# Two adaLN blocks of a trunk's down projection moved to general slots, and two low parts moved behind a mixing stage

## The chip, the cores and the metric

The kernel runs on one core of a Trainium2 chip. Its engines work side by side, each on its own list of instructions, in an order that is fixed when the program is built: PE multiplies matrices, DVE (vector) and ACT (scalar) do the work element by element, POOL does a few memsets and DMA issues, SP issues nearly all DMAs. They wait for each other through semaphores. The metric is the device time of one execution in microseconds; lower is better. All times below are in us unless they say ns.

## What is computed

A trunk of two layers over 512 tokens of width 1024. Layer 0 mixes tokens by a stick-breaking attention, layer 1 by a gated MLP that mixes positions inside chunks. Each mixer is followed by a SwiGLU FFN (width 2816), and each of the four sub-layers is wrapped in norms that a conditioning vector `c` shifts, scales and gates (adaLN):

```python
def ada_modulation(c, w, b):
    m = jax.nn.silu(c) @ w + b
    shift, scale, gate = jnp.split(m, 3, axis=-1)
    return shift[:, None, :], scale[:, None, :], gate[:, None, :]
...
def token_mixing_mixer(h, w_in, ln_g, w_s, b_s, w_out):
    uv = jax.nn.gelu(h @ w_in)
    u, v = jnp.split(uv, 2, axis=-1)
    v = layer_norm(v, ln_g)
    ...
    sv = jnp.einsum('gts,bnsgc->bntgc', ws, v) + b_s.T[None, None, :, :, None]
    y = u * sv.reshape(B, S, D)
    return y @ w_out

def swiglu(h, w_gate, w_up, w_down):
    return (jax.nn.silu(h @ w_gate) * (h @ w_up)) @ w_down
...
    for i in range(DEPTH):
        shift, scale, gate = ada_modulation(c, mix_ada_w[i], mix_ada_b[i])
        h = rms_norm(x, mix_pre_g[i]) * (1.0 + scale) + shift
        ...
        x = x + gate * rms_norm(y, mix_post_g[i])
        shift, scale, gate = ada_modulation(c, ffn_ada_w[i], ffn_ada_b[i])
        h = rms_norm(x, ffn_pre_g[i]) * (1.0 + scale) + shift
        y = swiglu(h, ffn_w_gate[i], ffn_w_up[i], ffn_w_down[i])
        x = x + gate * rms_norm(y, ffn_post_g[i])
```

## The kernel before

**Numbers in two parts.** Every fp32 operand is split into a high part that PE takes as it is (`wh`, `hTh`, `as`'s first half) and a low part, the rest (`wl`, `hTl`). A product is three matmuls: high by high, high by low, low by high (`mm3`). ACT makes the high part by a copy, DVE the low part by a subtraction, so each weight block costs one operation on either engine.

**Stages.** Attention; its output projection; gate and up of FFN0; the down projection of FFN0 (22 blocks `f` of 128 rows, each for 4 token tiles and 2 halves of the width); the mixing layer (`gmlp`); gate, up and down of FFN1. Each projection back to the width is `out_proj`: it loops over the blocks, the last four of them (the tail) per token tile, and after each tile `boundary` does the residual, the norms and the transposes (`tp`) for the next stage. In the first down projection, the sums of token tile 0 are set aside after block `mid - 1` (`yp`, `mid` = 13), because PSUM banks are needed.

**Weights.** `stream` lists all weight blocks in the order of use. `wload` issues the DMA of one into `raw` (2 buffers), `wemit` splits it into `wh`, `wl` (6 buffers), `wget` takes it. Gate and up columns of most FFN blocks, and two pairs of columns of the mixing layer's `u`, are computed with seven products in place of eight; their weights come as two loads, `rawx` (in `raw`) and `rawy` (in `raw2`, another pool of 2 buffers), and `blocks` (L255 on) builds sums of them, among others `b21`, a high and a low part of half of `rawy`.

**adaLN.** A `Bg` object spreads the matrix-vector products of adaLN over other work. Its name A, B or G stands for scale, shift and gate, the figure for the sub-layer. Each step issues one 512 KB load of ada weights (`rawada`) and, `lag` steps later, one multiply-add on DVE that uses it. After eight such products per part, the sum is split, PE adds over the partitions by a matmul with ones (`adaps`) and the row of norm gains `g` is put on. With `slots` of 0 the loads go to `raw2`; otherwise they go to the general slots, a pool of 28 tiles of 4 KB per partition (`slot`) that nearly everything else lives in as well. With `flat`, the parts follow each other without a pause to drain the lag.

In the first down projection two of them run: `bg` (A1, B1 and G2, in general slots, two steps per block, done by block 12) and `bg2` (A2 and B2, in `raw2`, lag 1). A2 and B2 are needed only at the boundary after the mixing layer; their last part (`adaps`) is done inside that layer.

**The mixing layer.** It computes `v` and `u`, normalises `v` (the statistics end in `r`, the variable `normed`), and for each of eight groups m: `sv` matmuls on PE, four `svt` operations on DVE, one product with `u`, and a split into `as`, on which the first output products (`part`) run. While it does so, weights of what follows are prepared.

**Order.** Inside the gate and up stages the order on PE, DVE and ACT is written out (`chain`). Elsewhere, a scheduler at build time sets the order on each engine from the program's order as priority, readiness and free buffers; an operation far back in the program may go early when its inputs and a buffer are there. `order(b, before)` keeps `b` behind another operation of the same engine without a semaphore. The low part of `b21` has such an order: for the `u` pairs behind the last sum of `v`'s weights (`summed`), for the first blocks of FFN1 behind `normed`.

The lines that the change and the prediction's steps touch: the low part of `b21` (L297 to L299), the steps of `bg2` in `out_proj` (L653, L654), `yp` (L656), `normed` (L1615), the end of the mixes (L1678 to L1681), and the making of `bg2` (L1694).

Of the kernel before, what the change touches and what calls it, by code (L numbers as in the profile page):

```python
# [15 lines left out]
NT = T // P  # L16
# [19 lines left out]
def trunk(ctx: ExitStack, tc: tile.TileContext, A: dict, out: bass.AP):  # L36
# [17 lines left out]
    def nm(s):  # L54
        uid[0] += 1
        return f"{s}_{uid[0]}"

    def slot(dt, name, a=2, b=512):
        return s4.tile([P, a, b], dt, tag="s4", name=nm(name))
# [21 lines left out]
    dve = Vector()  # L81
# [21 lines left out]
    def order(b, before):  # L103
        tc.add_manual_dep(
            b.ins, before.ins.name,
            mybir.DependencyInfo(mybir.DependencyClass.NoSync, mybir.DependencyReason.DATA),
            reason="order",
        )
# [28 lines left out]
    stream = []  # L137
    got = []
# [1 line left out]
    wpools = [(wpool, 5)]  # L140
    fwork = {}
    last_low = [None]
    last_block, summed, normed = [None], [None], [None]

    raws = []

# [43 lines left out]
    def wtile(a, b, at=0):  # L190
        turn[0] = (turn[0] + 1) % sum(c for _, c in wpools)
        pool = wpools[0][0] if turn[0] < wpools[0][1] else wpools[1][0]
        if at is SHORT:
            at = SHORT[turn[0] % 2]
        return [
            pool.tile([P, 1088], F32R, tag=n, name=nm(n))[:, at : at + a * b].rearrange(
                "p (a b) -> p a b", a=a
            )
            for n in ("wh", "wl")
        ]  # L200
# [57 lines left out]
    def blocks(xr, yr):  # L258

        fp = fwork["pool"]  # L260

        def high(t, src):
            act.activation(t[0][:], src, AF.Copy)

        def low(t, src):
            return dve.tensor_tensor(t[1][:], src, t[0][:].bitcast(F32), ALU.subtract)

        def half(t, i):
            return lambda k: (t[0][:, 4 * i + k, :], t[1][:, 4 * i + k, :])

        x = wtile(KD, P, SHORT)
        high(x, xr[:])
        f13 = fp.tile([P, KD, P], F32, tag="f13", name=nm("f13"))
        sum13 = dve.tensor_tensor(
            f13[:].rearrange("p (a k) f -> p a (k f)", a=2),
            xr[:].rearrange("p (a k) f -> p a (k f)", a=2),
            yr[:, 4:8, :].rearrange("p (a k) f -> p a (k f)", a=1).to_broadcast([P, 2, 512]),
            ALU.add,
        )
        if len(got) == first_blocks[-1]:  # L280
            order(sum13, feature[0])
        yield
        b21 = [
            fp.tile([P, 544], F32R, tag=f"b21{i}", name=nm("b21"))[
                :, SHORT[0] : SHORT[0] + 512
            ].rearrange("p (a b) -> p a b", a=4)
            for i in range(2)
        ]
        high(b21, yr[:, 0:4, :])
        t13 = wtile(KD, P, SHORT)  # L290
        high(t13, f13[:])
        f24 = fp.tile([P, KD, P], F32, tag="f24", bufs=1, name=nm("f24"))
        dve.tensor_tensor(f24[:, 0:4, :], f13[:, 0:4, :], xr[:, 4:8, :], ALU.add)
        dve.tensor_tensor(f24[:, 4:8, :], f24[:, 0:4, :], yr[:, 0:4, :], ALU.add)
        yield
        low(x, xr[:])
        b = low(b21, yr[:, 0:4, :])  # L297
        if normed[0] is not None:
            order(b, (summed if stream[len(got)][3][1][0] == "u" else normed)[0])  # L299
        yield  # L300
        t24 = wtile(KD, P, SHORT)
        high(t24, f24[:])
        low(t13, f13[:])
        yield
        low(t24, f24[:])
        got.append({
            "B11": half(x, 0), "B22": half(x, 1), "B21": half(b21, 0),
            "T1": half(t13, 0), "T3": half(t13, 1), "T2": half(t24, 0), "T4": half(t24, 1),
        })
# [308 lines left out]
    def out_proj(s, nk, get_act, wkey, J, bg, hT, nxt=(), pre=None, S=None, steps=0, bg2=None):  # L618

        last = 0 if steps else 3
        mid = min(nk - J, -(-8 * len(bg.parts) // steps) + 1) if steps else None
        yp = None
        y = [[None, None] for _ in range(NT)]

        def step(k, tt, a, w, halves=(0, 1)):
            for hf in halves:  # L630
                if k == 0 or k == mid and tt == last:
                    y[tt][hf] = bank("y", "p" if tt == last else "b")
                mm3(
                    y[tt][hf][:],
                    a[0][:, tt * P : (tt + 1) * P], a[1][:, tt * P : (tt + 1) * P],
                    w[0][:, 0, hf * 512 : (hf + 1) * 512],
                    w[1][:, 0, hf * 512 : (hf + 1) * 512],
                    k == 0 or k == mid and tt == last, k == nk - 1 or k + 1 == mid and tt == last,
                )

        npre = 0
        if pre is not None:
            npre = len(pre["w"])
            for tt in pre["y"]:
                y[tt] = pre["y"][tt]
        for k in range(nk - J):
            a = get_act(k)
            w = pre["w"][k] if k < npre else wget(wkey(k))
            for tt in range(NT):
                if k >= npre or tt not in pre["y"]:  # L650
                    step(k, tt, a, w)
            bg.step(steps)
            if bg2 is not None and k >= mid - 3 and k != mid - 1:  # L653
                bg2.step(4 if k < mid else 2)  # L654
            if k + 1 == mid:
                yp = slot(F32, "yp")  # L656
                for hf in range(2):
                    act.activation(yp[:, hf, :], y[last][hf][:], AF.Copy)
                bg.step(99)
        bg.step(99)  # L660
        tail = [
            (k, get_act(k), wget(wkey(k), J + 1 if k == nk - J else 0))
            for k in range(nk - J, nk)
        ]
        sqrt_table()
        xs = {tt: x_load(tt) for tt in range(2)}
        xin = xs.get
        for tt in range(NT):
            for hf in range(2):
                for k, a, w in tail:  # L670
                    step(k, tt, a, w, (hf,))
            if tt == last and yp is not None:
                for hf in range(2):
                    dve.tensor_tensor(yp[:, hf, :], y[tt][hf][:], yp[:, hf, :], ALU.add)
                y[tt] = [yp[:, hf, :] for hf in range(2)]
            if tt < 2:
                boundary(s, tt, y[tt], xin, hT, S, "p" if last == 0 else "b")
                xs[tt + 2] = x_load(tt + 2)
        evacs, late = [], []
        for n, tt in enumerate((2, 3)):  # L680
            def mid():
                edge[0] = True
                evacs.append(nxt[1]())
                edge[0] = False

            if nxt and tt == 2:
                evacs.append(nxt[0]())
            late.append(
                boundary(
                    s, tt, y[tt], xin, hT, S, "p" if tt == 3 else "b",  # L690
                    mid if nxt and tt == 3 else None,
                )
            )
        if nxt:
            evacs.append(nxt[2]())
            with tc.issue_after(last_sqrt[0].ins):
                for f in evacs:
                    f()
        if hT is not None:
            for f in late:  # L700
                f()
# [201 lines left out]
    with tc.tile_pool(name="att", bufs=1) as att, tc.tile_pool(name="att2", bufs=2) as att2:  # L903
# [58 lines left out]
        B31, B2, B0 = (3, 1), (2,), (0,)  # L962
# [582 lines left out]
    def gmlp(bg, hT, nhT, nS, nxt):  # L1545
# [66 lines left out]
        sd = small.tile([P, 52], F32, tag="sd4", bufs=1, name=nm("sd4"))[:, :NT]  # L1612
        act.activation(sd, mv[:, :, 1], AF.Sqrt, bias=epsb[:])
        r = small2.tile([P, 48], F32, tag="r4", bufs=1, name=nm("r4"))
        normed[0] = dve.reciprocal(r[:, :NT], sd)  # L1615
        vn = []
        for tt in range(NT):
            dve.tensor_scalar(
# [31 lines left out]
        def part(k):  # L1650

            w = wget(("wout", k), 2)
            pre["w"].append(w)
            for tt, y in pre["y"].items():
                for hf in range(2):
                    if k == 0:
                        y[hf] = bank("y", "p" if tt == 3 else "b")
                    c = slice(hf * 512, (hf + 1) * 512)
                    tok = slice(tt * P, (tt + 1) * P)
                    mm3(  # L1660
                        y[hf][:], sp[k][0][:, tok], sp[k][1][:, tok],
                        w[0][:, 0, c], w[1][:, 0, c], k == 0, False,
                    )
# [14 lines left out]
        for m in range(3, KD):  # L1678
            mixed(m)
            if m > 3:  # L1680
                part(m - 4)  # L1681
        out_proj(
            2, KD, lambda k: sp[k], lambda k: ("wout", k), 4, bg, nhT, nxt, pre, nS,
        )
# [6 lines left out]
        0, KD, lambda k: (o8[k][:, 0, :], o8[k][:, 1, :]), lambda k: ("wo", k),  # L1691
        4, bg, hT1, f0.first(), early, S1,
    )
    bg2 = Bg("A2", "B2", lag=1, gap=3)  # L1694
    f0.run(
        Bg("G1", slots=1), Bg("A1", "B1", "G2", slots=3, lag=2, flat=True), bg2, 2, hT2,
        [lambda: v_first(hT2, (0, 1)), lambda: v_first(hT2, (2, 3)), lambda: u_first(hT2)], S2,
# [107 lines left out]
```

## Time and profile before

| | us |
|---|---|
| median of 3 runs | 1103.92 |
| lowest and highest run | 1100.98, 1109.13 |
| the profiled execution | 1103.49 |
| its span, first to last instruction | 1101.7 |

The mean granted clock of PE in the profiled execution is 0.998 of full speed. Its stages, read from the profile's table of windows:

| stage | from, to | PE busy | DVE busy | DMA share |
|---|---|---|---|---|
| start and attention | 0 to 245 | 234.0 | 203.5 | 0.82, then 0.36 |
| output projection | 245 to 278 | 32.9 | 24.1 | 0.36 |
| FFN0 gate and up | 278 to 497 | 218.4 | 200.2 | 0.43 |
| FFN0 down projection | 497 to 621 | 123.7 | 109.7 | 0.78 |
| mixing layer | 621 to 764 | 142.6 | 126.5 | 0.38 |
| FFN1 gate and up | 764 to 980 | 215.8 | 198.2 | 0.37 |
| FFN1 down projection | 980 to 1101.7 | 114.6 | 110.5 | 0.32 |

How to read the lines below. In the table of windows: from and to, length, then for PE, PEld (weight loads of PE), DVE, ACT and POOL the busy time and in brackets the number of instructions, then the granted clock, the busy share of the DMA engines and GB/s. In a timeline: start, length, engine, line, operation, the tile it writes and those it reads, shape, number of merged instructions, and in square brackets how long the engine had been idle before and what ended that. In the chain that ended last: start, length, engine and tile; it is followed back from the last instruction, at each step to what released it. Matmuls are pipelined, so that PE's pace is read from the distance of their starts, or from their number in a window, rather than from the length of one. A name like `as<-act` is the tile written and the tile read.

### The profile page before, as it was taken

Reading aid. Unit: us, or ns where it says so; the run is one execution under the profiler, and the core shown is the slowest. Engines: PE = TensorE matmul, PEld = TensorE weight load, DVE = VectorE, ACT = ScalarE, POOL = GpSimd, SP = SyncE. Lnnn points to the kernel's source line nnn. Section 1 sums busy time; section 2 is a strip of 40 time slices with the busy share of each in tenths; the row PEclk is TensorE's granted clock in tenths of the full one; section 3 lists DMA queues with packets and bytes.
Section 4 is the critical chain, followed back from the end, with each engine's and each line's share of the span. In section 5 each row is a group of like instructions: output and inputs, shape, how many; then the busy total and the mean of one; then the engine's idle time right before and its main releaser. Section 6 shows DMA issues by size and latency. Waiting matters only on the chain.

```text
span 1101.7 us, 18701 instructions
## 1 busy us (share of the span) xinstructions
PE 1082.1 (98%) x7452; PEld 978.7 (89%) x7452; DVE 972.8 (88%) x1293; ACT 610.1 (55%) x1016; POOL 29.5 (3%) x53
## 2 busy tenths in 40 slices
PE   7999999999999999999999999999999999999997
PEld 4787788788999999998888899988999999999996
DVE  4988999866989999989978999868979999899996
ACT  6554665665655555554252767526545555565662
POOL 0020100000000000001000000001000000000000
PEclk9999999999999999999999999999999999999999
DMA  8976434304433434359878324524334342332252
GB/s 317 357 226 218 138 121 131 122 17 153 153 111 124 163 124 153 134 187 347 294 246 322 143 87 137 177 95 163 122 113 153 136 159 100 107 113 96 77 190 78
DMA packets 51355, 176.38 MB, mean 160 GB/s; under 512 B 6074, under 2 KB 9146, under 8 KB 51268
## 3 DMA queue, kind: packets, MB, share of 16 engines
q1 hardware_dynamic: 48708, 166.81, 43.8%
q0 software_dynamic: 2560, 8.39, 2.1%
q8 instruction: 58, 0.95, 0.3%
q14 instruction: 29, 0.24, 0.1%
HBM read 164.69 MB, written 8.39 MB: 157 GB/s over the span
## 4 chain that ended last, share of the span: by engine, by line
PE 85%; DVE 7%; DMA 4%; issue 2%; ACT 2%; SPq 0%; DVEq 0%; ACTq 0%
PE r L111 35%; PE y L111 16%; PE pqk L111 7%; PE X L111 4%; PE gu L111 4%; PE Y L111 3%; PE v L111 3%; PE u L111 2%; PE av L111 2%; PE z L111 2%; PE tw L119 1%; PE Z L111 1%; PE W L111 1%; PE tp L119 1%; DVE wl L184 1%
## 5 line engine op out<-in xcount | busy, mean ns | idle before, releaser
L111 PE MATMUL r<-Sh,wh 128*128 128x256 f32 x640 | 177.3, 277 | 0.6 <-ACT e L89 0.6
L111 PE MATMUL r<-Sl,wh 128*128 128x256 f32 x640 | 177.0, 277 | 0.0
L111 PE MATMUL r<-Sh,wl 128*128 128x256 f32 x640 | 176.9, 277 | 0.0
L89 ACT ACTIVATE wh<-raw 128x1024 fp32r<-128x1024 f32 (+1 forms) x105 | 108.3, 1036 | 101.7 <-DMA raw<-in_wdown 36.1
L111 PE MATMUL y<-wh,as 128*128 128x512 f32 x480 | 150.5, 391 | 0.3 <-DVE svt L73 0.3
L111 PEld LDWEIGHTS r<-Sh,wh 128*128 128x128 f32 x640 | 120.2, 188 | 1.2 <-ACT e L89 1.0
L111 PEld LDWEIGHTS r<-Sl,wh 128*128 128x128 f32 x640 | 120.2, 188 | 0.1
L111 PEld LDWEIGHTS r<-Sh,wl 128*128 128x128 f32 x640 | 120.1, 188 | 0.0
L184 DVE TENSOR_TENSOR wl<-raw,wh 128x1024 fp32r<-128x1024 f32 x79 | 95.9, 1220 | 25.9 <-ACT wh L89 25.7
L73 DVE TENSOR_TENSOR wl<-f,wh 128x1024 fp32r<-128x1024 f32 x95 | 112.9, 1219 | 1.1 <-ACT wh L89 1.1
L89 ACT ACTIVATE wh<-f 128x1024 fp32r<-128x1024 f32 x95 | 100.2, 1055 | 17.3 <-DVE f L73 12.5
L111 PEld LDWEIGHTS y<-wh,as 128*128 128x128 f32 x480 | 90.0, 188 | 19.3 <-issue 0.6
L89 ACT ACTIVATE e<-r 128x256 f32<-128x256 f32 x120 | 45.9, 384 | 102.3 <-PE r L111 100.2
L111 PE MATMUL y<-wl,as 128*128 128x512 f32 x240 | 93.7, 391 | 0.0
L111 PE MATMUL r<-hTh,wh 128*128 128x256 f32 x320 | 88.8, 278 | 0.2 <-DVE gu L73 0.2
L111 PE MATMUL r<-hTh,wl 128*128 128x256 f32 x320 | 88.5, 277 | 0.0
L111 PE MATMUL r<-hTl,wh 128*128 128x256 f32 x320 | 88.5, 277 | 0.0
L111 PEld LDWEIGHTS r<-hTh,wh 128*128 128x128 f32 x320 | 60.1, 188 | 1.1 <-DVE gu L73 0.9
L111 PE MATMUL r<-hTh,b 128*128 128x256 f32 x320 | 60.9, 277 | 0.0
L111 PEld LDWEIGHTS r<-hTl,wh 128*128 128x128 f32 x320 | 60.1, 188 | 0.0
L111 PEld LDWEIGHTS r<-hTh,wl 128*128 128x128 f32 x320 | 60.1, 188 | 0.0
L89 ACT ACTIVATE wh<-rawx 128x1024 fp32r<-128x1024 f32 x40 | 42.5, 1062 | 29.7 <-PE r L111 28.9
(288 smaller groups left out, 2924.3 us busy)
## 6 DMA issues: line engine op xcount, KB each, us to landing
rawada<-in_ada SPq DMA_DIRECT2D x80, 512.0 KB, 6.3
rawy<-in_wy SPq DMA_DIRECT2D x38, 512.0 KB, 4.2
rawx<-in_wx SPq DMA_DIRECT2D x38, 512.0 KB, 3.4
raw<-in_wdown SPq DMA_DIRECT2D x22, 512.0 KB, 5.3
raw<-in_wdn SPq DMA_DIRECT2D x22, 512.0 KB, 3.4
raw<-in_wqk SPq DMA_DIRECT2D x16, 512.0 KB, 4.0
ada<-in_ada0p SPq DMA_DIRECT2D x12, 512.0 KB, 7.6
raw<-in_wgu SPq DMA_DIRECT2D x12, 512.0 KB, 3.5
```

Of the source, the lines that this page charges most:

```text
L73: b = getattr(nc.vector, op)(*args, **kw)
L89: b = nc.scalar.activation(*args, **kw)
L111: b = nc.tensor.matmul(o, l, r, start=start, stop=stop, skip_group_check=True)
L119: last_tp[0] = nc.tensor.transpose(o, i, ident)
L184: last_low[0] = nc.vector.tensor_tensor(l[:], raw[:], h[:].bitcast(F32), ALU.subtract)
```

## The change

Two things are changed.

1. `bg2` (A2, B2) gets `slots=2, lag=2, flat=True`: its loads go to general slots, each product comes two steps after its load, and B2 follows A2 without a pause. Its 18 steps run at blocks 9 to 15 (1, 3, 3, 2, 3, 3, 3) and no longer at blocks 10, 11 (4 each) and 13 to 17 (2 each).
2. The low parts of `b21` of FFN1's blocks are ordered behind the last DVE operation of the mixes (`mixes`), and no longer behind the statistics of `v` (`normed`). The `u` pairs keep their order.

```diff
-    last_block, summed, normed = [None], [None], [None]
+    last_block, summed, mixes = [None], [None], [None]
...
         b = low(b21, yr[:, 0:4, :])
-        if normed[0] is not None:
-            order(b, (summed if stream[len(got)][3][1][0] == "u" else normed)[0])
+        after = summed if stream[len(got)][3][1][0] == "u" else mixes
+        if after[0] is not None:
+            order(b, after[0])
...
             bg.step(steps)
-            if bg2 is not None and k >= mid - 3 and k != mid - 1:
-                bg2.step(4 if k < mid else 2)
+            if bg2 is not None and mid - 4 <= k < mid + 3:
+                bg2.step((1, 3, 3, 2, 3, 3, 3)[k - mid + 4])
...
-        normed[0] = dve.reciprocal(r[:, :NT], sd)
+        dve.reciprocal(r[:, :NT], sd)
...
             if m > 3:
                 part(m - 4)
+        mixes[0] = dve.prev
         out_proj(
...
-    bg2 = Bg("A2", "B2", lag=1, gap=3)
+    bg2 = Bg("A2", "B2", slots=2, lag=2, gap=3, flat=True)
```

## The prediction

> **What bounds the kernel now.** I read the page first, then the table of windows, then the chain that ended last, then the timelines around its stops.
>
> ```profile
> span 1101.7 us, 18701 instructions
> ...
> PE 1082.1 (98%) x7452; PEld 978.7 (89%) x7452; DVE 972.8 (88%) x1293; ACT 610.1 (55%) x1016; POOL 29.5 (3%) x53
> ```
>
> PE is busy for 98% of the span, so only its few gaps, and any stretch where its matmuls come slower than they could, can be won. The change works in the first down projection (about 496 to 621 us) and in the mixing of the next layer (about 697 to 730 us). The 20 us windows of the down projection, where x is the number of matmuls on PE:
>
> ```profile
> 500.00:520.00 20.00, 20.00 (x90) 16.58 (x89) 19.77 (x19) 7.91 (x11) 0.95 (x1) 1.00 0.92 334
> 520.00:540.00 20.00, 20.00 (x90) 16.58 (x89) 18.89 (x19) 6.39 (x9) 1.79 (x2) 1.00 0.94 348
> 540.00:560.00 20.00, 20.00 (x90) 16.57 (x89) 17.47 (x15) 3.95 (x5) 0.12 (x1) 1.00 0.76 263
> 560.00:580.00 20.00, 20.00 (x88) 16.18 (x87) 15.78 (x22) 12.60 (x21) 0.00 (x0) 1.00 0.65 221
> 580.00:600.00 20.00, 20.00 (x90) 16.57 (x89) 16.13 (x16) 5.32 (x5) 0.00 (x0) 1.00 0.89 315
> 600.00:620.00 20.00, 19.74 (x96) 16.09 (x95) 18.28 (x29) 13.16 (x33) 1.61 (x3) 1.00 0.47 181
> ```
>
> PE starts 90 matmuls per 20 us, 0.222 us each, whether DVE is busy 19.77 or 16.13 us of a window and whether DMA is at 0.94 or 0.76: here it waits for nobody. One block f of the projection is 4 token tiles x 2 halves x 3 products = 24 matmuls, 24 x 0.222 = 5.33 us. The chain leaves PE in this stage all the same, because it ends in a late transpose:
>
> ```profile
> 598.11 0.06 DVE B L73
> 598.17 1.14 issue
> 599.31 1.23 DVE wl L184
> 600.55 0.33 SPq L128
> 600.88 0.05 issue
> 600.93 4.36 DMA rawy<-in_wuy
> 605.32 0.64 ACT b L89
> 605.95 1.05 ACT junk L89 x2
> ...
> 608.89 1.09 PE tp L119 x8
> ```
>
> Read upwards: the first token tile's transposes (tp) wait for its norm, the norm for the sum of squares on ACT (junk), that stands behind the rounding of b21 (b), which waits for rawy; on SP rawy stood behind a load that waited for a weight's low part (wl), and that ran on DVE after the last B2 product, which held the raw2 buffer that rawy takes. How much of that PE feels:
>
> ```profile
> 607.79 0.62 PE L111 MATMUL y<-wh,as 128*128 128x512 f32 x2
> 608.24 0.39 PE L111 MATMUL y<-wl,as 128*128 128x512 f32 x1
> 608.89 1.09 PE L119 MATMUL tp<-identt,t 128*128 128x128 f32 x8 [0.26 <-DVE t L73]
> ```
>
> Two matmuls start from 607.79 to 608.24, 0.225 us each; the one at 608.24 takes 0.65 us to the next start, so PE lost 0.65 - 0.225 = 0.42 us.
>
> **The change, part by part.**
>
> *A2/B2 (L654, L1694).* The 18 steps (16 loads and 16 multiply-adds, with the lag) stay 18; they go from f = 10, 11, 13 to 17 to f = 9 to 15. So 16 loads on SP, 16 DVE operations, two POOL memsets and two bias loads are neither added nor removed. The last product moves two blocks forward, 2 x 5.33 = 10.7 us, from 598.11 to about 587. DVE has room for that: it idles 20 - 17.47, 20 - 15.78 and 20 - 16.13, together 10.6 us, between 540 and 600. PE doesn't follow (its rate above), so this shift in itself is worth nothing; its cover is that weights and operands are ready ahead, and if the cover goes the price is that of the rivals.
>
> *raw2 freed.* A2/B2 no longer use the two raw2 buffers, so the two rawy loads of the u pairs can go any time after the first gate/up stage, and their two b21 roundings on ACT leave the boundary. What that is worth comes from these rows of DVE and ACT:
>
> ```profile
> 604.10 1.28 DVE L73 SCALAR_TENSOR_TENSOR x<-t,r,x 128x1024 f32<-128x1024 f32 x1
> ```
> ```profile
> 605.32 0.64 ACT L89 ACTIVATE b<-rawy 128x512 fp32r<-128x512 f32 x1 [1.45 <-DMA rawy<-in_wuy]
> 605.85 1.04 ACT L89 ACTIVATE junk<-x 128x1024 bf16<-128x1024 f32 x1
> ```
>
> x was there at 604.10 + 1.28 = 605.38; junk began at 605.85, 0.47 us late, for b alone. Without b the transposes could start at 608.89 - 0.47 = 608.42, before the matmul of 608.24 has given way (608.47): the whole 0.42 us goes. More can't be won here, for PE comes to the transposes only then; late next is PE's own order. The two rawy loads land earlier among the down weights: 2 x 0.524 MB at the 348 GB/s of the full window is 3.0 us, covered by the weights' lead (11.8 us for f = 17, rival C). In general slots the 16 ada loads are bounded by slots, not by raw2, and no row shows how SP would use that; bounds: -0.42 us (wait gone) to rival C's +3.3.
>
> *b21 lows behind the last mix (L298, L1682).* Two DVE operations of 0.68 us move, nothing is added but the order.
>
> ```profile
> 691.62 0.68 DVE L73 TENSOR_TENSOR b<-rawy,b 128x512 fp32r<-128x512 f32 x1
> ...
> 696.29 0.68 DVE L73 TENSOR_TENSOR b<-rawy,b 128x512 fp32r<-128x512 f32 x1
> 697.36 0.48 DVE L73 SCALAR_TENSOR_TENSOR svt<-sv,cols,bsb 128x256 f32<-128x256 f32 x1 [0.38 <-PE sv L111]
> ...
> 731.92 1.23 DVE L184 TENSOR_TENSOR wl<-raw,wh 128x1024 fp32r<-128x1024 f32 x1 [1.79 <-ACT wh L89]
> ```
>
> These are FFN1's two. After the second DVE still waited 0.38 us for PE before the first mix, so the lows stood in nobody's way: I take 0. At their new place DVE idles 1.79 us before one operation; two lows, 1.36 us, fit in it. Queued behind them there are the low parts of the wout weights; the waiting costs them nothing while that idle time lasts. Best case, from PE's rows in the mixing:
>
> ```profile
> 713.85 0.39 PE L111 MATMUL y<-wh,as 128*128 128x512 f32 x1
> 714.49 0.47 PE L111 MATMUL y<-wh,as 128*128 128x512 f32 x1 [0.26 <-DVE svt L73]
> ```
>
> 0.64 - 0.225 = 0.42 us lost to DVE; at best it goes. Worst case the two lows land in front of the next boundary: +1.36 us. The range keeps both; 0 is nearer to the row of 697.36.
>
> **Sum.** -0.42 + 0 + 0 = -0.4 us. The profiled execution took 1103.49 us for its span of 1101.7; it becomes 1103.1. The median shown, 1103.92, is 0.43 above it, so the median becomes 1103.5.
>
> **A rule against the row.** The Trainium skill's "Perfetto Trace Analysis", section "Identifying the Most-Contended Engine", holds matmul busy time for a poor measure and points to the share of LDWEIGHTS: here 16.58 of 20 us, 83%, which read as headroom leaves 17% in this stage. The trace does not agree: three windows in a row have exactly 90 matmuls, with different loads on DVE and DMA. That reading is rival D below.
>
> **Rivals.**
>
> *A. Nothing to measure.* The wait for b21 goes, but the scheduler, with other loads in front, puts another small ACT or DVE operation there; 0.4 us returns: 1103.9.
>
> *B. A late operand.* The operand of block 13 is the tightest of the stage.
>
> ```profile
> 557.75 2.60 DVE L73 SCALAR_TENSOR_TENSOR A<-rawada,sc,A 128x1024 f32<-128x1024 f32 x2
> 563.41 2.50 DVE L73 TENSOR_TENSOR as<-act,as 128x512 fp32r<-128x512 f32 x4 [3.07 <-ACT as L89]
> ...
> 576.60 1.22 DVE L184 TENSOR_TENSOR wl<-raw,wh 128x1024 fp32r<-128x1024 f32 x1
> ```
> ```profile
> 561.58 1.28 ACT L89 ACTIVATE yp<-y 128x512 f32<-128x512 f32 x2 [5.01 <-PE y L111]
> ```
>
> yp starts when PE has finished tile 0 of block 12; three tiles, 18 x 0.222 = 4.0 us, remain, so block 13 starts about 565.6. The first of the four lows is done at 563.41 + 0.68 = 564.1: a lead of 1.5 us. A product of A2 in front of it, as step f = 12 has two where it had none, costs 2.60 / 2 = 1.30 us; DVE's idle 3.07 us and the lead cover 4.6 us. Six of them in front, 7.8 us, delay PE by 3.2 us: 1107.1. For it: 1.5 us is little. Against: six more at one place is much.
>
> *C. Slower: a burst of ada loads.* With general slots nothing but free slots holds SP back. At 348 GB/s a 512 KB load takes 0.524 / 0.348 = 1.51 us. Block 17's weights are ready at 576.60 + 1.22 = 577.8; PE needs them four blocks after block 13 began, with the 12 broadcast matmuls of A1, B1 and G2 between: 565.6 + 4 x 5.33 + 12 x 0.222 = 589.6, a lead of 11.8 us. Ten loads in front cost 15.1 - 11.8 = 3.3 us (1107.2); all sixteen 24.1 - 11.8 = 12.3 us: 1116.2. More than 1% it is only if all sixteen go in front. For it: DMA at 0.94. Against: the products free slots in order, and DMA falls to 0.65 by 560.
>
> *D. Faster.* Were PE held back throughout by late operands, its 22 x 24 = 528 matmuls could go at the 16.58 / 89 = 0.186 us that a weight load takes: 528 x 0.036 = 19 us, 1085. The even rate speaks against it.
>
> **How the numbers follow.** Forecast 0.50; A 0.25; B 0.13; C 0.10 (0.04 with nearly all loads in front); D 0.02. One per cent, 11 us, is about what a measurement of this kernel can tell from no change: faster is D, 0.02; slower is the tail of C, 0.04; the rest, 0.94, lies within. The runs before lie between 1100.98 and 1109.13, which is wider than every term. The range reaches down to the lowest run less the best of the terms, 1100.98 - 0.42 - 0.42 = 1100.1, rounded down to 1099.5, and up to B with the worst of the lows, 1107.1 + 1.4 = 1108.5; ten loads of C lie within.
>
> **What will show it.** Right: no b21 rounding on ACT between 600 and 606 and rawy loads long before; no idle time before tp; the last product of B2 about 587; the two lows after the last mix, in DVE's idle time; 90 matmuls per window as before. Wrong: fewer than 88 matmuls in a window between 560 and 600 (B or C), a wait of PE on as or wl there, or the lows at the next boundary.

## The result, and the profile after

| | before | after |
|---|---|---|
| median of 15 runs each, same chip | 1103.58 | 1108.52 |
| lowest and highest | 1100.98, 1109.13 | 1106.96, 1110.48 |
| the profiled execution | 1103.49 | 1106.96 |
| its span | 1101.7 | 1105.2 |

The ratio after to before is 1.0046, with a 95% interval of 1.0035 to 1.0057. The change makes the kernel about 5 us slower. The forecast was 1103.5, the upper end of the range 1108.5. In the experiments below, two single executions, of 2790.2 us (`table_raw2`) and 3820.52 us (`no12`), stand far outside all others; they are in the medians given there, but not in the ratios.

The page of the changed kernel begins like that of before, with the same numbers of instructions on the engines. The totals don't show what happened:

```profile
span 1105.2 us, 18691 instructions
...
PE 1083.3 (98%) x7452; PEld 977.5 (88%) x7452; DVE 972.9 (88%) x1293; ACT 610.7 (55%) x1016; POOL 29.5 (3%) x53
```

The table of windows does (the columns are those of the prediction's table: PE, PEld, DVE, ACT and POOL busy with the number of instructions, granted clock, DMA share, GB/s):

```profile
540.00:560.00 20.00, 20.00 (x90) 16.54 (x89) 17.09 (x16) 2.64 (x3) 0.96 (x1) 1.00 1.03 410
560.00:580.00 20.00, 17.54 (x72) 12.83 (x71) 11.85 (x16) 9.54 (x16) 0.00 (x0) 1.00 0.45 171
580.00:600.00 20.00, 20.00 (x90) 16.56 (x89) 16.98 (x19) 7.96 (x11) 0.00 (x0) 1.00 0.51 176
600.00:620.00 20.00, 19.81 (x95) 16.06 (x94) 17.44 (x27) 11.88 (x29) 1.08 (x2) 1.00 0.45 166
```

One window of 20 us has 72 matmuls where it had 88, 16 x 0.222 = 3.6 us. The windows on both sides are as before. In the same window DVE is busy for 3.9 us less (11.85 after 15.78), ACT for 3.1 us less: this is no overload of an engine. PE's timeline of the changed kernel shows what PE stood for (start, length, engine, line, operation, written tile and read tiles, shape, number; in brackets how long PE had been idle and what ended that):

```profile
564.74 0.40 PE L111 MATMUL adaps<-acch,ones 128*128 128x512 f32 x1
564.98 0.39 PE L111 MATMUL adaps<-accl,ones 128*128 128x512 f32 x1
565.86 0.51 PE L111 MATMUL adaps<-acch,ones 128*128 128x512 f32 x1 [0.49 <-ACT acch L89]
566.58 0.50 PE L111 MATMUL adaps<-accl,ones 128*128 128x512 f32 x1 [0.22 <-DVE accl L73]
567.82 0.50 PE L111 MATMUL y<-wh,as 128*128 128x512 f32 x1 [0.75 <-ACT as L89]
...
572.88 0.39 PE L111 MATMUL y<-wh,as 128*128 128x512 f32 x1
574.25 0.49 PE L111 MATMUL adaps<-acch,ones 128*128 128x512 f32 x1 [0.98 <-ACT acch L89]
574.77 0.50 PE L111 MATMUL y<-wh,as 128*128 128x512 f32 x1
```

The distances of these starts, less the 0.23 of an undisturbed step, are 0.65, 0.49, 1.01, then 1.14 and 0.29 us: 3.6 us in two places. That the two spans differ by as much (3.5 us) is in part chance: this execution of after came to the stage earlier than that of before, and loses some more behind it (see what stays open). In the kernel before, the same broadcast matmuls (`adaps`, the sums over partitions of A1, B1 and G2) stand in PE's list with products between them:

```profile
566.15 0.40 PE L111 MATMUL adaps<-acch,ones 128*128 128x512 f32 x1
566.38 0.39 PE L111 MATMUL adaps<-accl,ones 128*128 128x512 f32 x1
566.61 0.39 PE L111 MATMUL y<-wh,as 128*128 128x512 f32 x1
...
567.54 0.39 PE L111 MATMUL adaps<-acch,ones 128*128 128x512 f32 x1
```

ACT tells the same from the other side. First the timeline of before, then that of after:

```profile
562.75 3.74 ACT L89 ACTIVATE as<-act 128x512 fp32r<-128x512 f32 x7
566.58 0.63 ACT L89 ACTIVATE acch<-A 128x512 fp32r<-128x512 f32 x1
```
```profile
561.37 1.09 ACT L89 ACTIVATE yp<-y 128x512 f32<-128x512 f32 x2 [7.94 <-PE y L111]
565.17 0.63 ACT L89 ACTIVATE acch<-A 128x512 fp32r<-128x512 f32 x1 [2.72 <-PE adaps L111]
566.62 0.63 ACT L89 ACTIVATE acch<-B 128x512 fp32r<-128x512 f32 x1 [0.82 <-DVE accl L73]
567.16 0.61 ACT L89 ACTIVATE as<-act 128x512 fp32r<-128x512 f32 x1
```

Before, seven operand copies follow `yp` at once, and the broadcasts' halves come behind them. After, ACT has two halves ahead of the operand of block 13. It waits 2.72 us until the broadcast matmul of 564.74 has read the only `acch` tile (there is one `acch` and one `accl`), then 0.82 us for the low half, and only then makes `as`. PE's list is fixed: behind the first broadcast stand the second and then the product that needs this `as`. So three engines take turns, as the chain of waits says (start, length, what):

```profile
564.90 0.25 PE adaps L111
...
565.17 0.64 ACT acch L89
...
565.84 0.70 DVE accl L73
...
566.62 0.63 ACT acch L89
567.25 0.53 ACT as L89
...
567.82 3.03 PE y L111 x12
```

The second place, at 574.25 us, is alike: PE waits there for the next half, which ACT makes only at 573.57 us, behind two copies of `B` and a weight's high part.

DVE, which the prediction had watched, stands idle through the first:

```profile
555.96 1.28 DVE L73 SCALAR_TENSOR_TENSOR A<-rawada,sc,A 128x1024 f32<-128x1024 f32 x1
565.84 0.69 DVE L73 TENSOR_TENSOR accl<-A,acch 128x512 fp32r<-128x512 f32 x1 [8.60 <-ACT acch L89]
```

What remained to be settled was which part of the change moves the lists, and whether the order, the loads or the slots are to blame.

### The profile page after: what moved, and what is told of

The parts are those of the page before. It is cut to its first block, busy times and chain, and to the rows that moved or that the text cites. A ratio compares the mean times of both kernels' runs of the same rounds, so it can differ in the third digit from the quotient of the medians.

```text
span 1105.2 us, 18691 instructions
## 1 busy us (share of the span) xinstructions
PE 1083.3 (98%) x7452; PEld 977.5 (88%) x7452; DVE 972.9 (88%) x1293; ACT 610.7 (55%) x1016; POOL 29.5 (3%) x53
## 4 chain that ended last, share of the span: by engine, by line
PE 88%; DVE 5%; ACT 3%; DMA 2%; issue 1%; SPq 0%; DVEq 0%; ACTq 0%
PE r L111 34%; PE y L111 18%; PE pqk L111 7%; PE v L111 6%; PE X L111 4%; PE gu L111 4%; PE Y L111 3%; PE av L111 2%; PE z L111 2%; PE tw L119 1%; PE Z L111 1%; PE W L111 1%; PE tp L119 1%; PE ab L111 1%; DVE wl L184 1%
```

## The experiments

All ratios are to the kernel before, run on the same chip in the same set, with 95% intervals. "PE's loss" in a stretch is worked out from the timeline: the distances of the matmuls' starts less their undisturbed pace, summed. Between 560 and 580 us it is 0.36 us in before and 4.1 us in after.

**Either part alone.** `only_steps` has the change of `bg2` with the old order of the lows; `only_lows` has the new order of the lows with the old `bg2`.

```diff
# only_steps, against after
-        after = summed if stream[len(got)][3][1][0] == "u" else mixes
-        if after[0] is not None:
-            order(b, after[0])
+        if normed[0] is not None:
+            order(b, (summed if stream[len(got)][3][1][0] == "u" else normed)[0])
# only_lows, against after
-            if bg2 is not None and mid - 4 <= k < mid + 3:
-                bg2.step((1, 3, 3, 2, 3, 3, 3)[k - mid + 4])
+            if bg2 is not None and k >= mid - 3 and k != mid - 1:
+                bg2.step(4 if k < mid else 2)
...
-    bg2 = Bg("A2", "B2", slots=2, lag=2, gap=3, flat=True)
+    bg2 = Bg("A2", "B2", lag=1, gap=3)
```

> The kernel before with the first part of the change alone: A2/B2 in general slots, two ahead, over blocks 9 to 15; the low parts of b21 stay where they were. Slots theory (the loads in general slots leave no slot for the operand of block 13 when the order is made, so it comes behind broadcast work and PE waits): 4 to 5 us slower than before, PE's stops between 563 and 575 us as in the changed kernel. Table theory (the steps at blocks 9 to 12 crowd the work before yp, whatever buffer they use): the same. Lows theory (the low parts behind the last mix cost the time, around 680 to 720 us): no difference from before.

> The kernel before with the second part alone: low parts of FFN1's first b21 blocks behind the last mix; A2/B2 as before. Slots and table theories: within 1 us of before, no stop of PE near 565 us. Lows theory: 1 to 5 us slower, with PE's stops at 680 to 720 us longer than before.

Measured: `only_steps` 1108.86, ratio 1.0040 (1.0025 to 1.0055); `only_lows` 1104.99, ratio 1.0005 (0.9995 to 1.0016). The waits of PE between 560 and 590 us in `only_steps` (engine and line, what was waited for, us in total, times, longest):

```profile
PE adaps L111 <- ACT acch L89: 1.5, 2, 1.0
PE y L111 <- ACT as L89: 0.7, 1, 0.7
PE adaps L111 <- DVE accl L73: 0.2, 1, 0.2
```

These are the waits of after. The lows cost nothing that can be measured, in either direction; the loss is in the first part. The window of `only_steps` shows one thing more:

```profile
560.00:580.00 20.00, 17.55 (x65) 12.71 (x64) 9.19 (x12) 7.08 (x12) 0.00 (x0) 0.91 0.46 178
```

PE starts 65 matmuls there, 7 fewer than in after, because the granted clock falls to 0.50 for 3.4 us from 569.91 us, just behind the first stops; the matmuls then start 0.43 us apart. That is some 1.6 us on top of the stops. The profile of `b2_raw2`, below, has the same for 3.4 us from 611.57 us, behind a wait before the transposes. In after, `paced` and `operand_first` the clock stays at 1.00 behind their stops, so it happens in some executions only; what decides it isn't shown.

**Slots or steps.** `slots_old_table` keeps the general slots, the lag and `flat`, with the old steps; `table_raw2` keeps the new steps, with the loads in `raw2` and a lag of 1. Both have the old order of the lows.

```diff
# slots_old_table, against only_steps
-            if bg2 is not None and mid - 4 <= k < mid + 3:
-                bg2.step((1, 3, 3, 2, 3, 3, 3)[k - mid + 4])
+            if bg2 is not None and k >= mid - 3 and k != mid - 1:
+                bg2.step(4 if k < mid else 2)
# table_raw2, against only_steps
-    bg2 = Bg("A2", "B2", slots=2, lag=2, gap=3, flat=True)
+    bg2 = Bg("A2", "B2", lag=1, gap=3)
```

> The kernel before with A2/B2 in general slots, lag 2 and flat, but at the old steps (four at blocks 10 and 11, two each at 13 to 17). Slots theory: 4 us slower, PE waits near 565 us. Table theory: within 1 us of before.

> The kernel before with the new table of steps alone (1, 3, 3, 2, 3, 3, 3 at blocks 9 to 15), still in raw2 with lag 1 and a pause between A2 and B2. Slots theory: within 1 us of before, the operand of block 13 straight behind yp. Table theory: 4 us slower, PE waits for that operand near 565 us.

Measured: `slots_old_table` 1105.99, ratio 1.0011 (1.0000 to 1.0022), PE's loss 1.1 us, with one wait left (PE y on ACT as, 0.5 us); `table_raw2` 1106.75, ratio 1.0013 (0.9998 to 1.0027), loss 0.65 us, and outside that stretch a wait of 1.5 us before the first transposes. Neither has the 4 us: it takes the new steps together with the general slots (and the lag of 2 and `flat`, which came with the slots; no run takes these apart).

**Where the loads lie.** `b2_raw2` leaves A2 in general slots and puts B2's loads into `raw2`. `hold12` is the kernel before with twelve of the 28 general slots held empty from block 9 until the broadcast of G2 is done (582 us).

```diff
# b2_raw2, against after
-                        if self.slots:
+                        if self.slots and not (self.gap == 3 and j >= KD):
# hold12, against before
             bg.step(steps)
+            if bg2 is not None and k == mid - 4:
+                holds = [slot(F32, "hold") for _ in range(12)]
+                for t in holds:
+                    nc.gpsimd.memset(t[:], 0.0)
...
+                for t in holds if bg2 is not None else ():
+                    dve.tensor_copy(t[:, 0, 0:1], ada["G", 2][:, 1023:1024])
```

> The changed kernel with B2's loads back in raw2 and A2's in general slots. Slots theory: B2's loads no longer sit in slots, the operands of blocks 13 to 18 come together behind yp, loss at 560 to 580 us under 1.5 us, 3 us faster than the changed kernel, though the late first transposes near 609 us may come back (0.4 to 2 us). Without it: 3 to 4 us of loss stay.

> The kernel before (A2/B2 in raw2, old steps) with twelve general slots taken by tiles that hold nothing, from early in the stage until G2's broadcast is done (about 578 us); costs twelve memsets on POOL, which idles, and twelve copies of one column on DVE, about 0.1 us each. Slots theory: the shortage alone makes operands of blocks 13 on late, PE loses 1.5 to 4 us between 560 and 580 us that it doesn't lose before. If the shortage isn't it: under 1 us of loss there, within 1.5 us of before.

Measured: `b2_raw2` 1109.72, ratio 1.0042 (1.0029 to 1.0055), loss 2.6 us at the same place, and 2.1 us before the first transposes at 609. `hold12` 1105.76, ratio 1.0015 (1.0002 to 1.0029); it waits up to 1.3 us before the transposes, but its window has as many matmuls as that of before:

```profile
560.00:580.00 20.00, 20.00 (x88) 16.12 (x87) 19.85 (x24) 10.77 (x17) 0.96 (x1) 1.00 0.86 291
```

So neither B2's loads in the slots nor a mere want of slots makes the stop. The Trainium skill, in "Perfetto Trace Analysis", section "Optimization Strategy", says that gaps which repeat can mean that there isn't room in SBUF for the next tile. For the general slots `hold12` does not bear it out here; for one small pair of tiles `acc2_27`, below, does in part.

**Fewer steps at block 12.** `no12` takes the two steps at block 12 and puts them into blocks 13 and 14.

```diff
-                bg2.step((1, 3, 3, 2, 3, 3, 3)[k - mid + 4])
+                bg2.step((1, 3, 3, 0, 4, 4, 3)[k - mid + 4])
```

> The changed kernel with the table 1, 3, 3, 0, 4, 4, 3: no step of A2/B2 in block 12, so that no load of B2 stands in the program ahead of block 13's operand. Slots theory: the operand comes straight behind yp, the loss at 565 us falls under 1.5 us, 3 us faster than the changed kernel. If it is the run of steps as a whole that matters, the loss stays at 3 to 4 us.

Measured: 1106.96, ratio 1.0017 (1.0007 to 1.0028). Over half of the loss goes with the two steps there. In the program as built the first group of four broadcasts on PE is gone, but a later one is there (place 3647 of PE's list, where after has its group at 3623). Its profile is of the execution of 3820.52 us, so where the rest lies isn't shown.

**Operands ahead of the broadcasts.** `operand_first` splits the operands of blocks 10 to 14 before the steps of block 9; `operands_17b` splits those of blocks 13 to 17 at the end of block 12.

```diff
# operands_17b, against after
+        held = {}
         for k in range(nk - J):
-            a = get_act(k)
+            a = held.pop(k) if k in held else get_act(k)
+            if bg2 is not None and k == mid - 1:
+                held = {i: get_act(i) for i in range(k + 1, mid + 5)}
# operand_first: the same with
+            if bg2 is not None and k == mid - 4:
+                held = {i: get_act(i) for i in range(k + 1, mid + 2)}
```

> The changed kernel, with the operands of blocks 10 to 14 split ahead of the steps of block 9, so that they take their general slots before the loads of A2 and B2 do. Slots theory (loads of A2/B2 in the slots that the operands of blocks 13 and 14 need): PE's loss between 560 and 580 us falls from 4.1 to under 1.5 us, and the time is 3 us or more below the changed kernel. Broadcast theory (PE waits there for the chain of acch, adaps, accl with its single buffer, whatever the operands do): 3 to 4 us of loss stay.

> The changed kernel, with the operands of blocks 13 to 17 split at the end of block 12, ahead of the broadcasts (five slots are held for it). In the program as built five operand copies then stand ahead of yp on ACT, and on PE the broadcast matmuls stand in ones and twos between products where the changed kernel has four in a row. Theory 1 (the order built: operands behind the broadcasts, so that the broadcast matmuls of several halves stand in a row on PE and wait for a single buffer): PE's loss between 560 and 600 falls from about 4 us to under 1.5, and the time to about 1104 to 1106. Theory 2 (shortage of slots on the chip, through the loads that run ahead): holding five more slots makes it worse, 1109 or more, with waits of PE on wl or as between 580 and 610.

Measured: `operand_first` 1109.17, ratio 1.0037 (1.0024 to 1.0050). The stop was not cured; it moved back by ten to twenty microseconds, to where PE's list has three broadcast matmuls in a row (place 3667) and what follows them. The waits between 560 and 590 us:

```profile
PE y L111 <- DVE G L73: 1.3, 1, 1.3
PE y L111 <- DVE as L73: 1.1, 1, 1.1
PE adaps L111 <- ACT acch L89: 0.7, 1, 0.7
...
```

`operands_17b` 1103.89, ratio 0.9999 (0.9990 to 1.0008). Its list of waits of PE between 560 and 600 us is empty, and the windows are those of before, though DVE and ACT idle even more than in after:

```profile
560.00:580.00 20.00, 20.00 (x88) 15.99 (x87) 10.63 (x13) 6.79 (x12) 0.00 (x0) 1.00 0.67 256
```
```profile
566.78 0.63 ACT L89 ACTIVATE acch<-A 128x512 fp32r<-128x512 f32 x1 [3.69 <-PE adaps L111]
```

ACT still waits for the broadcast (3.69 us). But the operands of blocks 13 to 17 are no longer behind it, and PE has products between the broadcasts:

```profile
566.35 0.40 PE L111 MATMUL adaps<-acch,ones 128*128 128x512 f32 x1
566.59 0.39 PE L111 MATMUL adaps<-accl,ones 128*128 128x512 f32 x1
566.82 0.39 PE L111 MATMUL y<-wl,as 128*128 128x512 f32 x1
...
567.52 0.46 PE L111 MATMUL adaps<-acch,ones 128*128 128x512 f32 x1
```

The lists as built, from `yp` on ACT, and the groups of broadcast matmuls on PE (place in the list and length of the group), say it before any run:

```text
ACT  before        yp yp as as as as as as as acch as as acch acch B
     after         yp yp acch acch as acch B wh B acch as acch acch
     operands_17b  (as as as as as as wh) yp yp acch acch acch B wh B
     acc2_27       yp yp acch acch as acch B B acch wh acch as
PE   before        3623 x2, 3629 x1, 3634 x1, 3637 x1, 3645 x1, 3648 x1
     after         3623 x4, 3639 x2, 3644 x1, 3647 x1, 3649 x1
     operands_17b  3627 x2, 3632 x1, 3637 x1, 3653 x2, 3658 x1
     acc2_27       3623 x4, 3637 x2, 3640 x2, 3644 x2, 3648 x1
```

**Loads that run ahead.** On the chip, SP in after issues the loads of A2 and B2 early, up to five in a row, and from 540 to 560 us the DMA engines move 410 GB/s where it was 263. `paced` holds each of these loads behind the weight load ahead of it in the program and leaves the groups of broadcasts on PE as they are in after.

```diff
-                        load(raw, A["ada"][s, part, j % KD])
+                        b = load(raw, A["ada"][s, part, j % KD])
+                        if s == 2 and self.gap == 3:
+                            order(b, last_load[0])
```

> The changed kernel, with each A2/B2 load held on its queue behind the weight load issued before it in the program, so that the loads can't run ahead of the weights. The order on PE around the broadcasts is the same as in the changed kernel (four in a row). Theory 1 (the order built): the stops at 565 to 568 and 574 stay, loss between 560 and 580 of 3.5 us or more, time 1108 to 1109. Theory 2 (loads that run ahead on the chip take slots and the queue): they go, loss under 1 us, time 1104 to 1105.

Measured: 1109.20, ratio 1.0044 (1.0031 to 1.0057), PE's loss 4.0 us, the four stops of the same lengths (the last, of 0.98 us, at 576.69):

```profile
568.31 0.50 PE L111 MATMUL adaps<-acch,ones 128*128 128x512 f32 x1 [0.49 <-ACT acch L89]
...
570.27 0.50 PE L111 MATMUL y<-wh,as 128*128 128x512 f32 x1 [0.75 <-ACT as L89]
```

The stops are where the order is that of after. The edit did not lower the peak, though: 540 to 560 us is at 410 GB/s in `paced` too, so this run can't tell the order from the loads. `slots_old_table` can: it moves 400 GB/s from 540 to 560 us, in another order, and loses 1.1 us. `operands_17b` has the same loads in its program as after and loses nothing, but its peak is lower, 335 GB/s.

**A second buffer.** `acc2_27` gives the second half of each broadcast an `acch` and `accl` of its own, paid for with one general slot.

```diff
-    s4 = ctx.enter_context(tc.tile_pool(name="s4", bufs=28))
+    s4 = ctx.enter_context(tc.tile_pool(name="s4", bufs=27))
...
-                    h = adas.tile([P, 512], F32R, tag="acch", name=nm("acch"))
-                    l = adas.tile([P, 512], F32R, tag="accl", name=nm("accl"))
+                    h = adas.tile([P, 512], F32R, tag=("acch", "acch2")[b], name=nm("acch"))
+                    l = adas.tile([P, 512], F32R, tag=("accl", "accl2")[b], name=nm("accl"))
```

> The changed kernel, with a buffer of its own for the second half of each broadcast (acch, accl), paid for with one general slot (27 in place of 28). On PE the first four broadcast matmuls still stand in a row, on ACT two halves still stand ahead of block 13's operand. If the single buffer is what PE waits for (half, matmul, half, matmul), the stop of 0.49 and 0.22 us at 566 shrinks to one, and the loss between 560 and 580 falls from 4.1 to about 2 to 3 us: some 1107. If it is the operand behind the broadcasts alone, the loss stays at 3.5 us or more and the time at 1108 to 1109. The slot less may cost some tenths by itself.

Measured: 1105.40, ratio 1.0013 (1.0004 to 1.0022), loss 2.3 us. The four broadcasts in a row now run without a stop, the stop at 574 is gone, and the wait for the operand is what is left:

```profile
566.20 0.40 PE L111 MATMUL adaps<-acch,ones 128*128 128x512 f32 x1
566.43 0.39 PE L111 MATMUL adaps<-accl,ones 128*128 128x512 f32 x1
567.89 0.50 PE L111 MATMUL y<-wh,as 128*128 128x512 f32 x1 [1.07 <-ACT as L89]
```

With the second pair of tiles the loss is 1.8 us less, within what was expected, and the operand behind the halves makes most of the rest: 1.2 us at 567.89 for its high part, 0.4 at 569.97 for its low part. The time fell further than the expected 1107.

**The rounding alone.** `b21_late` is the kernel before with the one gain that the prediction counted on made by itself: the roundings of `b21` of the `u` pairs are ordered on ACT behind the last boundary's square.

```diff
-            act.activation(t[0][:], src, AF.Copy)
+            return act.activation(t[0][:], src, AF.Copy)
...
-        high(b21, yr[:, 0:4, :])
+        h = high(b21, yr[:, 0:4, :])
+        if stream[len(got)][3][1][0] == "u":
+            order(h, feature[1])
```

> The kernel before, with the rounding of b21 of the u pairs ordered on ACT behind the last boundary's square (nothing else is changed). It takes the wait ahead of the first transposes away without moving a load. The idle time before tp at about 608.9 goes, and with it 0.4 us by the profile of before, up to 2 us where other runs of the same order showed more: 1102 to 1103.6, so 0.998 to 0.9996 of the kernel before. Rival: the rounding lands in front of another boundary operation or the weights of u come late, and the time is the same or some tenths more.

Measured: 1104.86, ratio 1.0003 (0.9992 to 1.0014): no difference. The transposes still wait:

```profile
607.93 1.09 PE L119 MATMUL tp<-identt,t 128*128 128x128 f32 x8 [0.80 <-DVE t L73]
```

No version beat the kernel before.

## Why the prediction was wrong, point by point

**The step that failed** is the one on A2/B2: "PE doesn't follow (its rate above), so this shift in itself is worth nothing; its cover is that weights and operands are ready ahead, and if the cover goes the price is that of the rivals." The cover did go, for operands, and at the place the prediction had called the tightest, block 13; PE lost 3.6 us there and at the next half behind it. But the price was taken from a DVE queue: products of A2 ahead of the operand's low part. DVE had nothing ahead of it; it idled for 8.60 us. What was late was the operand's high part on ACT, behind two broadcast halves in a list made at build. The prediction took it, without saying so, for a fact of the stage that the operands are split ahead of the broadcasts; it was one result of the scheduler among others, and the change gave another. The prediction moved only the operations that the diff names and left the rest of each list where it was. `operands_17b` puts the operands back in front and returns the whole loss.

**Rival B** had the place, the sign and the size (1107.1, by 3.2 us), with 0.13, but not the mechanism: its own condition, six products ahead on DVE, never came about in after. (Something like it did in `operand_first`: there an operand's low part ran on DVE only at 587.36 us, behind products of B2, and PE waited 1.1 us for it.) A rival that is right only in its sum is a warning that the place was worth more thought than its likeliest mechanism.

**Rival C.** The burst came: SP's queue issued five ada loads in a row, the DMA share was 1.03 from 540 to 560 us, and the next weight load went out at 574.48 us:

```profile
535.13 6.11 SPq L128 DMA_DIRECT2D rawada<-in_ada  x5
...
556.45 3.84 SPq L128 DMA_DIRECT2D rawada<-in_ada  x3
574.48 0.33 SPq L128 DMA_DIRECT2D raw<-in_wdown  x1
```

No wait of PE on a weight followed; the window from 580 to 600 us has its 90 matmuls. Whatever the burst took of the lead of 11.8 us that the prediction worked out, the rest was enough.

**The gain of 0.42 us.** The mechanism was right as far as it went. No `b21` rounding is left in the boundary, and PE loses 0.23 us at the transposes where it lost 0.42:

```profile
610.11 0.61 PE L111 MATMUL y<-wh,as 128*128 128x512 f32 x2
610.79 1.10 PE L119 MATMUL tp<-identt,t 128*128 128x128 f32 x8
```

The second of the two matmuls starts at 610.11 + 0.225 = 610.34, and 610.79 - 610.34 - 0.225 = 0.23. "The whole 0.42 us goes" was too much. At the second tile's transposes (617.71) PE loses 0.29 us where it lost 0.06 in before, so over the two tiles nothing is won. And `b21_late` shows that the rounding by itself is worth nothing that can be measured: without it, the boundary's chain from the end of the second `yp` to the transposes takes 5.7 us in place of 6.1, but on DVE the chain still stands behind the last B2 product, which waits 2.36 us for its load, and PE waits 0.80 us. With the stops cured, `operands_17b` at 0.9999 (0.9990 to 1.0008) is the worth of the rest of the change.

**What was right.** The last B2 product moved forward (589.23, forecast about 587). The lows of `b21` stand in DVE's list behind the last mix's operation (732.61), followed by idle time, and `only_lows` prices them at nothing:

```profile
733.22 1.29 DVE L73 TENSOR_TENSOR b<-rawy,b 128x512 fp32r<-128x512 f32 x2
735.12 1.23 DVE L184 TENSOR_TENSOR wl<-raw,wh 128x1024 fp32r<-128x1024 f32 x1 [0.61 <-ACT wh L89]
```

The sign to look for, "fewer than 88 matmuls in a window between 560 and 600 (B or C), a wait of PE on as or wl there", named what came. Rival D, the headroom in the weight loads, got no support: PE's pace between the stops is the same 0.23 us.

**What stays open.** Why the scheduler puts the halves ahead of the operands. It takes the slots (with their lag and `flat`) and the new steps together, and the steps at block 12 have the larger part in it; neither B2's loads in the slots nor twelve slots fewer does it alone. No run shows which of its inputs tips it. Also, the medians of before and after are 4.9 us apart and the spans of the two profiles 3.5. The traces account for most of the difference: the first product of the down projection starts at 493.9 us in before and at 492.5 in after, so this execution of after, its fastest, was 1.4 us ahead (the order on every engine is the same in both up to 469 us), and from there to the end it loses 4.9. 3.7 of them are gone by 600 us. The other 1.1 lie in small waits behind, the longest ahead of the first output product of the mixing (716.55), which starts 0.86 us behind the matmul before it, against 0.28 in before. `b21_late`, which has neither part of the change, shows 0.64 there and `only_lows`, which has the second, 0.28, so it isn't shown that these belong to the change. The clock may add to the median: it is 0.997 on the mean in five of the fifteen executions of after, as a stretch like that of `only_steps` would make it (3.4 us at half the clock are 0.0015 of the span), and their median is 1109.92, that of the others 1108.18.

## What to carry to other kernels

Where a scheduler at build sets the order, a change of a background stream's buffers and steps is a change of every engine's list in that stage. Price it by the tightest operand on each engine that makes it, ACT as well as DVE, and compare the lists around that operand first: four broadcasts in a row in place of two was visible in the program. If a burst of small chains with a single buffer stands in a stage, put the operands of the next blocks ahead of it explicitly, or give the chain a second buffer; here the one returned all of the loss, the other about half of PE's loss in the stage and most of the time.

## What the runs showed that I had not expected

The wait before the first transposes varies with the same list on PE. In before it cost 0.42 us; in the profiled execution of `only_lows`, whose lists in that stage are those of before, 2.3 us, because the last B2 product waited 3.21 us for its load:

```profile
600.99 1.28 DVE L73 SCALAR_TENSOR_TENSOR B<-rawada,sc,B 128x1024 f32<-128x1024 f32 x1 [3.21 <-DMA rawada<-in_ada]
```

One profile's 0.42 us is thus one draw of that wait, and a forecast that rests on it should carry such a spread.
